# A hybrid decoder layer on one core: the input projection multiplies the raw rows, and the pooling sums run as a scan

## The chip, the cores and the metric

The kernel runs on one core of one Trainium2 chip. The metric is the device time of one execution in microseconds (us), lower is better; the time before is the median of three runs. The profile is one further execution, recorded by the hardware profiler.

## The reference, cut to what matters

One layer (`DEPTH` 1) over 512 rows (tokens) of width 1024: a root-mean-square norm, one wide projection, three mixers side by side (attention, causal pooling, a state-space scan), a merge, and a feed-forward part. The pooling windows w are 2, 4, 8 and 16, for 256 columns each. The change touches the norm, the pooling and the first uses of the projection:

```python
def rmsnorm(x, g):
    y = xf * lax.rsqrt(jnp.mean(xf * xf, axis=-1, keepdims=True) + NORM_EPS)
    return (y * g.astype(jnp.float32)).astype(x.dtype)
...
    u = rmsnorm(x, ln1_g[i])
    proj = u @ w_in[i]
    q, k, v, pool_in, z, xbc, dt_raw, gate_pre = jnp.split(proj, split_idx, axis=-1)
...
def pool_mixer(u, w_grp, scale):
    cs = jnp.cumsum(uf, axis=1)
    for gi, w in enumerate(POOL_WINDOWS):
        c = cs[..., sl]
        shifted = jnp.pad(c, ((0, 0), (w, 0), (0, 0)))[:, :s]
        cnt = jnp.minimum(pos, w).astype(jnp.float32)
        outs.append((c - shifted) / cnt - uf[..., sl])
```

The factor `rsqrt(...)` belongs to a row. It can be put on the row before the product with `w_in` or on the row of the result behind it; the two orders give the same product.

## The kernel before, in words

**Products.** Every float32 operand is split into a high part (a rounded copy) and a low part (what the rounding left). A product is three passes, high by high, high by low, low by high, in `mm3` (L230). Weights arrive by DMA as `raw`; ScalarE writes the high part `wh` (`cast`, L185) and VectorE the low part `wl` (`low`, L221, its line L217). There are two buffers for `raw`, three for `wh`, two for `wl`. A `Job` is one weight block with its products. At job n the loop at the end of the kernel (L1949) issues the low part of block n+1, the cast of n+2 and the load of n+3, and then the job's products. An output chunk of 128 features by 512 rows is 24 matmuls (8 slices of the inner dimension, three passes), and then its evacuation.

**Order.** The instructions of each engine run in the order in which the program issues them (`manual_schedule`, L104). Small pieces of work are generators in `running`; `step()` (L155) takes each one `yield` further, and is called once a chunk (once in two row blocks in the jobs for v). `after(n, it)` holds a piece back by n steps. So the position of a piece in an engine's queue is counted in steps.

**Buffers.** All tiles of 128x512 come from one pool of 52 (`T`, L106). PSUM has four banks "mm" for products (`MM`) and four "sm" for everything else (`SM`).

**Start.** The normed, transposed input is kept as `uh` (high) and `ul` (low), 8 slices of 128 features by 512 rows. For the first 256 rows (two blocks) the kernel sums the squares of a block, works out the factor and writes it on a diagonal (L1895); TensorE multiplies the block by it (`turn_scale`, L1882), which turns and scales it in one. ScalarE and VectorE then write `uh` and `ul` from PSUM (`turned`, L1851). Rows 256 to 511 are scaled in SBUF (L1919, L1921) and turned by plain transposes (L1932). Until the first product the chain is load, squares, factor, diagonal, turn, split. WARM matmuls on a tile of ones (L1825) run ahead of it.

**First two jobs.** The pooling's projection is four jobs of two chunks. The first two of these are issued by hand (`begin`, L1858): each half of the rows of each job by itself, so 192 matmuls of 256 columns (L1866). The other two go through the loop, with 512 columns a matmul (L239). Then come two jobs for v of the first attention group with the state-space step widths (`v_jobs`, L622, 400 columns), three jobs for q and k (`qk_jobs`, L692) and the pooling's own product (`pool_out_job`, L921).

**Pooling.** `pool_evac` (L895): ScalarE copies the chunk out of PSUM to `pu`; GpSimd doubles windows (add the tile shifted by 1, 2, 4, 8, with a copy of the first columns each, L904 and L905) and corrects the first columns by `ramp` (L907). Two steps later VectorE forms mean minus value (L913), ScalarE its high part (L915), VectorE its low part (L916).

`sums_of_u` (L403) adds `uh` and `ul` back together (L408) for sums that later jobs use. A table `col` of biases is turned by TensorE (`turn`, L505), and `parts_of_bias` prepares a table of attention biases.

Of the kernel before, what the change touches and what calls it, by code (L numbers as in the profile page):

```python
# [10 lines left out]
F32 = mybir.dt.float32  # L11
# [5 lines left out]
P = 128  # L17
S = 512
# [64 lines left out]
def trunk(ctx: ExitStack, tc, out, x, rel_bias, ln1_g, w_in, b_gate, w_a, pool_w, pool_scale, w_b,  # L83
# [318 lines left out]

    def sums_of_u(p):  # L403

        f = []
        for k in (2 * p, 2 * p + 1):
            f.append(T("uf"))
            dve.tensor_tensor(f[-1], uh[:, k, :].bitcast(F32), ul[:, k, :].bitcast(F32), OP.add)  # L408
# [206 lines left out]
        return plain(ap, 1) if g == 0 else perm(ap, g)  # L615

    dtr = cpool.tile([P, 4, SH], F32, name="dtr")

    both = cpool.tile([P, 4, 32 + HEADS], F32, name="nmls")
    V, QK, OT, NM, LS = {}, {}, {}, {}, {}  # L620

    def v_jobs(g):  # L622
        extra = SH if g == 0 else 0

        def parts(k0, k1):
            c = C_V + 384 * g
            r = [wsrc(w_in, k0, k1, c, c + 384)]
            if extra:
                r.append(wsrc(w_in, k0, k1, C_DT, C_DT + SH))
            return r  # L630

        def evac(tb, ps):
            t = T(f"v{g}")
            act.copy(t[:, :384], ps[:, :384])
            if extra:
                act.copy(dtr[:, tb, :], ps[:, 384:400])
            V[g, tb] = t

        return jobs_b(parts, 384 + extra, lambda k, tb: uh[:, k, tb * P:(tb + 1) * P],
                      lambda k, tb: ul[:, k, tb * P:(tb + 1) * P], KD, evac)  # L640

    def v_pair():

# [252 lines left out]
    def pool_evac(m, ps):  # L896
        g = m // 2
        w = 2 << g
        u = T("pu")
        act.copy(u, ps)  # L900
        cur, sh = u, 1
        while sh < w:
            nxt = T("psw")
            pool.tensor_tensor(nxt[:, sh:], cur[:, sh:], cur[:, :S - sh], OP.add)  # L904
            pool.tensor_copy(nxt[:, :sh], cur[:, :sh])  # L905
            cur, sh = nxt, sh * 2
        pool.tensor_tensor(cur[:, :w], cur[:, :w], ramp[:, g, :w], OP.mult)  # L907

        def later():
            yield  # L910
            yield
            d = T("pd")
            dve.scalar_tensor_tensor(d, cur, 1.0 / w, u, OP.mult, OP.subtract)  # L913
            dh, dl = T("pdh", F32R), T("pdl", F32R)
            act.copy(dh, d)  # L915
            dve.tensor_sub(dl, d, dh.bitcast(F32))  # L916
            DP[m] = (dh, dl)

        running.append(later())
# [892 lines left out]
    load_x(0, (sp, act))  # L1812
    act.dma_start(eye, c_eye)
    load_x(1, (sp, act))
    act.dma_start(g8[:KD, :P], ln1_g[0].rearrange("(k p) -> k p", p=P))
    dve.memset(ones.bitcast(F32), 1.0)
# [4 lines left out]
    first = [MM("pa") for _ in range(4)]  # L1821

    def warm_up(n):
        for i in range(n):
            pe.matmul(first[3][:, :P], ones.bitcast(F32), ones.bitcast(F32), start=True, stop=True)  # L1825

    fetch(weights[0], 2)
    fetch(weights[1])
# [8 lines left out]
    sp.dma_start(tri, c_tri)  # L1837
    rows_of_bias, parts_of_bias, second_table, residues_of_bias = bias_rows()

    def row_squares(tb, ss, n=1, eng=dve):  # L1840

        for i in range(n):
            squares(act, xin[tb + i, 0], ss[:, i:i + 1])
            squares(eng, xin[tb + i, 1], ss[:, n + i:n + i + 1])
        dve.tensor_tensor(ss[:, :n], ss[:, :n], ss[:, n:2 * n], OP.add)
        return ss[:, :n]

    def x_block(tb, k):
        return xin[tb, k // 4][:, (k % 4) * P:(k % 4 + 1) * P]

    def turned(k, lo, ps):  # L1851

        hh = uh[:, k, lo:lo + 256]
        act.mul(hh, ps, g1[:, k:k + 1])
        dve.scalar_tensor_tensor(ul[:, k, lo:lo + 256], ps, g1[:, k:k + 1], hh.bitcast(F32),
                                 OP.mult, OP.subtract)

    def begin(n, lo, hi, between=lambda early: None):  # L1858
        wh, wl = weights[n].split
        js = range(2)  # L1860
        order = [(wh, uh, k, j) for j in js for k in js]
        for k in range(2, KD + 2):
            order += [(wh, uh, k, j) for j in js if k < KD] + [(wh, ul, k - 2, j) for j in js]
        for part in (order, [(wl, uh, k, j) for j in (1, 0) for k in range(KD)]):
            for a, b, k, j in part:
                pe.matmul(first[2 * n + j][:, lo:hi], a[:, k, j * P:(j + 1) * P], b[:, k, lo:hi],  # L1866
                          start=a is wh and b is uh and k == 0, stop=a is wl and k == KD - 1)
            between(part is order)
        if hi == S:
            for j in range(2):  # L1870
                pool_evac(2 * n + j, first[2 * n + j])
                step()


    warm_up(WARM)
    diag = [T("diag") for _ in range(2)]
    banks = [SM("uT") for _ in range(4)]

    def bank(k):
        return banks[k % 4][:, (k // 4) * 256:(k // 4) * 256 + 256]  # L1880

    def turn_scale(tb, k):  # L1882
        pe.matmul(bank(k)[:, tb * P:(tb + 1) * P], x_block(tb, k), diag[tb][:, :P], start=True, stop=True)

    for tb in range(2):
        s0, s1, v, sq, r, rt = (small(n, [P, 1]) for n in ("s0", "s1", "v", "sq", "r", "rt"))
        squares(act, xin[tb, 0], s0)
        squares(dve, xin[tb, 1], s1)
        dve.tensor_scalar(v, s0, 1.0 / D, EPS, OP.mult, OP.add)
        act.activation(sq, s1, AF.Sqrt, bias=v, scale=1.0 / D)  # L1890
        dve.scalar_tensor_tensor(rt, s1, 1.0 / D, v, OP.mult, OP.add)
        dve.reciprocal(r, sq)
        dve.scalar_tensor_tensor(rt, r, rt, r, OP.mult, OP.mult)
        dve.tensor_scalar(rt, rt, -0.5, 1.5, OP.mult, OP.add)
        dve.tensor_scalar(diag[tb][:, :P], eye, r, rt, OP.mult, OP.mult)  # L1895
        if tb == 0:
            for k in range(KD):
                turn_scale(0, k)
    pe.transpose(first[2][:, :KD], g8[:KD, :P], eye[:KD, :KD])
    dve.tensor_copy(g1, first[2][:, :KD])  # L1900

    cast(weights[0], 2, other=dve)
    low(weights[0], 2, pool)
    for k in range(KD):
        turn_scale(1, k % 2 * 4 + k // 2)
    for k in range(KD):
        turned(k, 0, bank(k))
    cast(weights[1], 2)
    parts = lows(weights[1], 2)


    ss = row_squares(2, small("ss", [P, 4]), 2)
    next(parts)
    r = rstd_of(ss, 2, D)
    for tb in (2, 3):
        for h in range(2):
            t = xin[tb, h]
            if h:
                dve.tensor_scalar(t, t, r[:, tb - 2:tb - 1], None, OP.mult)  # L1919
            else:  # L1920
                act.mul(t, t, r[:, tb - 2:tb - 1])  # L1921
    next(parts)
    begin(0, 0, 256)

    def turns(early):
        if not early:
            return
        for k in range(4):
            banks[k] = SM("uT")
        for k in range(KD):  # L1930
            for tb in range(2):
                pe.transpose(bank(k)[:, tb * P:(tb + 1) * P], x_block(2 + tb, k), eye)  # L1932
        for k in range(KD):
            turned(k, 256, bank(k))

    begin(1, 0, 256, turns)
    turn()
    parts_of_bias()
    fetch(weights[2])
    fetch(weights[3])  # L1940
    begin(0, 256, S)
    cast(weights[2])
    low(weights[2])
    begin(1, 256, S)
    cast(weights[3])
    fetch(weights[4])


    n = 0  # L1949
    for job in jobs:  # L1950
# [2 lines left out]
            continue  # L1953
        while second:
            flush()
        if n >= 2:
            def prepare(n=n, later=False, spread=not job.once):

                def rest():
                    if n + 1 < len(weights):  # L1960
# [27 lines left out]
WARM = 12  # L1988

# [1 line left out]
_INS = ['x', 'rel_bias', 'ln1_g', 'w_in', 'b_gate', 'w_a', 'pool_w', 'pool_scale', 'w_b',  # L1991
# [26 lines left out]
```

## Time and profile before

| what | us |
|---|---|
| median of 3 runs (lowest, highest) | 1014.83 (1014.29, 1014.94) |
| profiled execution, its time | 1014.66 |
| its span in the trace | 1012.9 |
| TensorE busy (share of the span) | 1000.9 (99%) |
| VectorE | 734.6 (73%) |
| ScalarE | 527.0 (52%) |
| GpSimd | 153.3 (15%) |

In the lines of the profile PE is TensorE, PEld its weight loads, DVE VectorE, ACT ScalarE, POOL GpSimd, SP the engine that issues most DMAs. A group's line has line of code, engine, operation, output<-inputs, shapes, count, then busy time in us and the mean ns of one, then the idle time in front. A line of the timeline has the start, the time until the last of the run has ended, engine and operation, and in brackets the idle time before it and what ended that. A line of the chain of waits has start, length and what ran. A busy TensorE is not TensorE at its peak, since matmuls overlap.

### The profile page before, as it was taken

To read this page: it belongs to the slowest core of one execution; us is meant where nothing else is said; L and a number is where in the kernel's file an instruction comes from. 1 tells how busy PE (TensorE), PEld (TensorE's weight loads), DVE (VectorE), ACT (ScalarE), POOL (GpSimd) and SP (SyncE) were. 2 spreads that over 40 slices of the span, in tenths; PEclk is the share of its full clock that TensorE was granted. 3 is DMA by queue.
4 is the path that set the end of the run, shared out by engine and by line. 5 is a ranking of instruction groups with operands and counts; after the bars stand their busy time and mean duration, and the time that the engine had idled before them with its cause. 6 is when DMAs were issued, how large, how long until landed. Compare 5 with 4: busy or idle time off the path is not lost.

```text
span 1012.9 us, 13676 instructions
## 1 busy us (share of the span) xinstructions
PE 1000.9 (99%) x5360; PEld 853.6 (84%) x5360; DVE 734.6 (73%) x933; ACT 527.0 (52%) x894; POOL 153.3 (15%) x141
## 2 busy tenths in 40 slices
PE   8999999999999999999999999999999999999996
PEld 8998878999988888888888888898888888888885
DVE  6564768577767655776889888768778768685877
ACT  5433556454435566888576246554444434443454
POOL 1680010110000000000043501302111100121031
PEclk9999999999999999999999999999999999999999
DMA  8244270655352435552253754232252134542573
GB/s 246 81 105 136 86 206 5 175 165 146 94 166 81 115 95 142 142 132 62 82 153 117 219 188 88 82 125 85 91 201 83 46 117 149 178 115 73 146 180 111
DMA packets 117583, 126.76 MB, mean 125 GB/s; under 512 B 6771, under 2 KB 96438, under 8 KB 117519
## 3 DMA queue, kind: packets, MB, share of 16 engines
q1 hardware_dynamic: 111887, 116.39, 37.0%
q0 software_dynamic: 5040, 8.65, 5.4%
q8 instruction: 42, 0.69, 0.3%
q10 hardware_dynamic: 592, 0.86, 0.2%
q14 instruction: 22, 0.18, 0.1%
HBM read 121.30 MB, written 3.00 MB: 123 GB/s over the span
## 4 chain that ended last, share of the span: by engine, by line
PE 95%; DVE 3%; DMA 1%; issue 0%; ACT 0%; ACTq 0%
PE pa L239 36%; PE pu L239 23%; PE pb L239 9%; PE pd L239 8%; PE pqk L239 6%; PE pq L239 3%; PE pa L1866 2%; PE ps L781 1%; PE ppw L239 1%; PE po L829 1%; PE pt L815 1%; PE py L1114 1%; PE pu L1543 1%; DVE wl L217 1%; DMA xin<-in_x_dram 1%; PE pyo L1121 1%
## 5 line engine op out<-in xcount | busy, mean ns | idle before, releaser
L217 DVE TENSOR_TENSOR wl<-raw,wh 128x2048 fp32r<-128x2048 f32 (+3 forms) x86 | 205.9, 2394 | 42.3 <-ACT wh L195 33.9
L195 ACT CAST wh<-raw 128x1024 fp32r<-128x1024 f32 (+3 forms) x169 | 169.8, 1022 | 48.9 <-DVE raw L362 17.8
L1440 DVE SCALAR_TENSOR_TENSOR hc<-pu,fcol,hc 128x510 f32<-128x510 f32 x88 | 65.8, 748 | 53.1 <-ACT hc L1437 51.5
L239 PE MATMUL pa<-uh,wh 128*128 128x512 f32 (+1 forms) x368 | 88.8, 381 | 0.0
L239 PE MATMUL pa<-ul,wh 128*128 128x512 f32 (+1 forms) x368 | 86.8, 375 | 0.0
L239 PE MATMUL pa<-uh,wl 128*128 128x512 f32 (+1 forms) x368 | 86.8, 375 | 0.0
L239 PE MATMUL pu<-uh,wh 128*128 128x512 f32 (+1 forms) x352 | 83.6, 379 | 0.0
L239 PE MATMUL pu<-uh,wl 128*128 128x512 f32 (+1 forms) x352 | 83.5, 379 | 0.0
L239 PE MATMUL pu<-ul,wh 128*128 128x512 f32 (+1 forms) x352 | 83.5, 379 | 0.0
L239 PEld LDWEIGHTS pa<-ul,wh 128*128 128x128 f32 x368 | 66.7, 188 | 12.6
L239 PEld LDWEIGHTS pa<-uh,wl 128*128 128x128 f32 x368 | 66.7, 188 | 12.5
L239 PEld LDWEIGHTS pa<-uh,wh 128*128 128x128 f32 x368 | 65.3, 189 | 11.8
L239 PEld LDWEIGHTS pu<-ul,wh 128*128 128x128 f32 x352 | 64.2, 188 | 12.5
L239 PEld LDWEIGHTS pu<-uh,wl 128*128 128x128 f32 x352 | 64.2, 188 | 12.5
L239 PEld LDWEIGHTS pu<-uh,wh 128*128 128x128 f32 x352 | 64.1, 188 | 12.4
L1445 POOL TENSOR_TENSOR hc<-hc 128x512 f32<-128x512 f32 x22 | 29.9, 1360 | 279.3 <-DVE hc L1440 243.3
L1437 ACT ACTIVATE hc<-pu,fcol,fcol 128x512 f32<-128x512 f32 x40 | 31.2, 779 | 75.0 <-PE pu L239 75.0
L217 DVE TENSOR_TENSOR wl<-w,wh 128x2048 fp32r<-128x2048 f32 (+1 forms) x26 | 54.2, 2087 | 10.3 <-issue 4.6
L195 ACT CAST wh<-w 128x1024 fp32r<-128x1024 f32 (+1 forms) x52 | 47.2, 950 | 10.0 <-DVE x L1666 5.3
L803 ACT ACTIVATE sb<-sb,nmls 128x128 f32<-128x128 f32 (+1 forms) x72 | 30.0, 418 | 31.6 <-DVE nmls L800 20.9
L1097 POOL TENSOR_TENSOR st<-st,dts 128x512 f32<-128x512 f32 x4 | 4.2, 1050 | 225.5 <-ACT st L1105 165.6
L1442 ACT ACTIVATE hc<-hc 128x512 f32<-128x512 f32 x22 | 13.9, 632 | 40.3 <-DVE hc L1440 40.2
(436 smaller groups left out, 1964.4 us busy)
## 6 DMA issues: line engine op xcount, KB each, us to landing
raw<-in_w_in_dram SPq DMA_DIRECT2D x24, 1024.0 KB, 5.5
raw<-in_ffn_w_up_dram SPq DMA_DIRECT2D x22, 1024.0 KB, 5.1
raw<-in_w_in_dram SPq DMA_DIRECT2D x14, 512.0 KB
raw<-in_w_in_dram SPq DMA_DIRECT2D x8, 768.0 KB, 7.3
raw<-in_ffn_w_down_dram SPq DMA_DIRECT2D x6, 1024.0 KB, 5.1
raw<-in_w_b_dram SPq DMA_DIRECT2D x4, 1024.0 KB, 5.3
al<-ad SPq DMA_DIRECT2D x16, 256.0 KB, 6.8
raw<-in_w_c_dram SPq DMA_DIRECT2D x4, 1024.0 KB, 7.6
```

The lines of the kernel that those rows point to most:

```text
L195: (other.tensor_copy if other and i else act.copy)(job.high[:, :, o], job.raw[:, :, o])
L217: (eng or dve).tensor_tensor(l[:, :, o], job.raw[:, :, o], h[:, :, o].bitcast(F32), OP.subtract)
L239: pe.matmul(ps, l, r, start=first and n == 0, stop=last and n == total - 1, skip_group_check=onto)
L781: pe.matmul(pss[i][:, o:o + w * P], q[r, n * P:(n + 1) * P], k[r, kb * P:(kb + w) * P], start=True, stop=True)
L803: act.activation(sb[:, off:off + w * P], sb[:, off:off + w * P], AF.Exp, bias=nm[:, n, h:h + 1], accum_out=ls[:, n, h:h + 1])
L815: pe.transpose(pt[:, o:o + P], sb[:, o:o + P], eye)
L829: pe.matmul(po[DH * hh:DH * hh + DH, n * P:(n + 1) * P], V[g, kb + i][:, (2 * c + hh) * DH:(2 * c + hh + 1) * DH], probs[2 * c + hh, nb][: ...
L1437: act.activation(t, ps, AF.Identity, bias=ff["c1"][:, ff["b"] + m:ff["b"] + m + 1], scale=fw(2, m))
L1440: dve.scalar_tensor_tensor(t[:, sh:], ps[:, :S - sh], fw(k, m), t[:, sh:], OP.mult, OP.add)
L1442: act.activation(t, t, AF.Silu)
L1445: pool.tensor_tensor(a, a, t, OP.mult)
L1866: pe.matmul(first[2 * n + j][:, lo:hi], a[:, k, j * P:(j + 1) * P], b[:, k, lo:hi], start=a is wh and b is uh and k == 0, stop=a is wl and ...
```

## The change

1. The rows are turned as loaded: 32 plain transposes into PSUM, no diagonal. ScalarE and VectorE write the high and low parts `xh`, `xl` of x times the gain, one block of 128 rows and one slice at a time (`split_x`), in the order `TURN` = 0, 4, 1, 5, 2, 6, 3, 7, so that the two slices of one PSUM bank follow each other. `x_parts` takes 24 of the 52 tiles: `xh`, `xl`, `xf`.
2. The four pooling jobs and the two jobs for v multiply `xh`, `xl`. The rows' factor comes behind: as a row in all partitions (`rows["r"]`, by way of a transpose, a write to DRAM and a broadcast load) in `pool_evac`, and as a column (`rcol`) in the evacuation of v. The sums of squares move behind the splits.
3. Job 0 alone is issued by hand, both high-part passes ahead of the low part of the weights. Its weights arrive in two halves ahead of the other rows; VectorE casts the first half, ScalarE the second, GpSimd writes the low parts. Job 1 goes through the loop with 512 columns a matmul.
4. `pool_evac`: VectorE multiplies the chunk by the factor out of PSUM, and makes the running sum of the window by two scans, one over the first w columns, one that adds the new column and subtracts the one that leaves. Mean minus value comes four steps later, its low part a step after that.
5. `uh` and `ul` are written later, in `normed`: GpSimd multiplies `xf` (x times gain, whole) by the row of factors, ScalarE copies to `uh`, VectorE subtracts to `ul`, spread over ten steps. `xf` itself is written by GpSimd (first 256 rows) and ScalarE (others, from PSUM). `sums_of_u` of the first four slices uses `xf` and no longer adds.
6. The turn of `col` and `parts_of_bias` run in steps inside job 1 and job 2. WARM is 10 in place of 12.

The diff, cut:

```diff
     def sums_of_u(p):
-        f = []
-        for k in (2 * p, 2 * p + 1):
-            f.append(T("uf"))
-            dve.tensor_tensor(f[-1], uh[:, k, :].bitcast(F32), ul[:, k, :].bitcast(F32), OP.add)
+        if p < 2:
+            f = [xf[2 * p], xf[2 * p + 1]]
+        else:
...
+    def normed():
+        for k in range(0, KD, 2):
+            for i in (k, k + 1):
+                pool.tensor_tensor(xf[i], xf[i], rows["r"], OP.mult)
+                act.copy(uh[:, i, :], xf[i])
+            yield
+        yield
+        for k in range(0, KD, 2):
+            yield
+            for i in (k, k + 1):
+                dve.tensor_sub(ul[:, i, :], xf[i], uh[:, i, :].bitcast(F32))
     def v_jobs(g):
...
-            act.copy(t[:, :384], ps[:, :384])
+            act.mul(t[:, :384], ps[:, :384], rcol[:, tb:tb + 1])
...
     def pool_evac(m, ps):
         u = T("pu")
-        act.copy(u, ps)
-        cur, sh = u, 1
-        while sh < w:
-            nxt = T("psw")
-            pool.tensor_tensor(nxt[:, sh:], cur[:, sh:], cur[:, :S - sh], OP.add)
-            pool.tensor_copy(nxt[:, :sh], cur[:, :sh])
-            cur, sh = nxt, sh * 2
-        pool.tensor_tensor(cur[:, :w], cur[:, :w], ramp[:, g, :w], OP.mult)
+        dve.tensor_tensor(u, ps, rows["r"], OP.mult)
+        cur = T("psw")
+        dve.tensor_tensor_scan(cur[:, :w], ones.bitcast(F32)[:, :w], u[:, :w], 0.0, OP.mult, OP.add)
+        dve.tensor_tensor_scan(cur[:, w:], u[:, w:], u[:, :S - w], cur[:, w - 1:w], OP.add, OP.subtract)
+        dve.tensor_tensor(cur[:, :w], cur[:, :w], ramp[:, g, :w], OP.mult)
         def later():
+            for _ in range(4):
+                yield
+            dve.scalar_tensor_tensor(cur, cur, 1.0 / w, u, OP.mult, OP.subtract)
...
+            act.copy(dh, cur)
             yield
+            dve.tensor_sub(dl, cur, dh.bitcast(F32))
...
-        yield from jobs_a(w_in, C_POOL, 8, uhk, ulk, KD, pool_evac)
+        yield from jobs_a(w_in, C_POOL, 8, xhk, xlk, KD, pool_evac)
...
     act.dma_start(g8[:KD, :P], ln1_g[0].rearrange("(k p) -> k p", p=P))
+    sp.dma_start(eye, c_eye)
+    load_x(0, (act, sp))
...
+    load_x(1)
+    load_w0(0, 0, 8)
+    load_w0(1, 0, 8)
     load_x(2)
     load_x(3)
+    fetch(w1)
...
+    def turned(tb):
+        if tb % 2 == 0:
+            banks[:] = [SM("uT") for _ in range(4)]
+        o = tb % 2 * P
+        for k in TURN:
+            pe.transpose(bank(k)[:, o:o + P], xin[tb, k // 4][:, (k % 4) * P:(k % 4 + 1) * P], eye)
+
+    def split_x(tb, k):
+        o, c = tb % 2 * P, slice(tb * P, (tb + 1) * P)
+        act.mul(xh[k][:, c], bank(k)[:, o:o + P], g1[:, k:k + 1])
+        dve.scalar_tensor_tensor(xl[k][:, c], bank(k)[:, o:o + P], g1[:, k:k + 1],
+                                 xh[k][:, c].bitcast(F32), OP.mult, OP.subtract)
...
     warm_up(WARM)
     pe.transpose(first[2][:, :KD], g8[:KD, :P], eye[:KD, :KD])
+    turned(0)
     dve.tensor_copy(g1, first[2][:, :KD])
+    for k in TURN:
+        split_x(0, k)
+    turned(1)
+    for n, k in enumerate(TURN):
+        if n == 2:
+            for k0 in (0, 4):
+                dve.tensor_copy(h0[part(0, k0, k0 + 4)], raw0[part(0, k0, k0 + 4)])
+            low0(0, 0, KD)
+        split_x(1, k)
+    group(0, (HH,), 0, 256, TURN)
+    group(0, (HL,), 0, 256, TURN)
+    for k0 in (0, 4):
+        act.copy(h0[part(1, k0, k0 + 4)], raw0[part(1, k0, k0 + 4)])
+    low0(1, 0, KD)
...
+    group(1, (HH,), 0, 256)
+    turned(2)
+    for k in TURN:
+        split_x(2, k)
+    group(1, (HL,), 0, 256)
+    group(0, (LH,), 0, 256)
...
+    turned(3)
+    for k in TURN:
+        split_x(3, k)
+    group(1, (LH,), 0, 256)
+    fetch(weights[2])
...
+    both_high(256, S, (0, 1))
+    group(0, (LH,), 256, S)
+    group(1, (LH,), 256, S)
...
+    dve.tensor_tensor(ss[:, :4], ss[:, :4], ss[:, 4:], OP.add)
+    r = rstd_of(ss[:, :4], 4, D)
+    for j in range(2):
+        act.copy(w1.high[:, :, j * P:(j + 1) * P], w1.raw[:, :, j * P:(j + 1) * P])
+    dve.tensor_copy(rcol, r)
+    pe.transpose(first[2][:4, :P], rcol, eye)
...
+    sp.dma_start(rd.rearrange("(t p) -> t p", p=P), rt[:4, :P])
+    sp.dma_start(rows["r"], rd.partition_broadcast(P))
+    low(w1, 2)
+    cast(weights[2], 2)
+    fetch(weights[3])
     for k in range(KD):
+        act.mul(xf[k][:, 256:], bank(k), g1[:, k:k + 1])
     low(weights[2])
+    running.append(after(3, columns_of(turn)))
+    running.append(after(4, columns_of(parts_of_bias)))
+    for j in range(2):
+        pool_evac(j, first[j])
+        step()
+    running.append(normed())
```

More of the change, by code (lines that the diff above doesn't have):

```diff
@@ L1838, in trunk @@
     rows_of_bias, parts_of_bias, second_table, residues_of_bias = bias_rows()
[L1840 to L1872, printed above, removed]
@@ L1875, in trunk, with part, low0 @@
-    warm_up(WARM)
-    diag = [T("diag") for _ in range(2)]
-    banks = [SM("uT") for _ in range(4)]
+    h0 = w0.high = whp.tile([P, KD, 256], F32R, name="wh", tag="wh")
+    l0 = wlp.tile([P, KD, 256], F32R, name="wl", tag="wl")
+    w0.split = h0, l0
+    def part(j, k0, k1):
+        return slice(None), slice(k0, k1), slice(j * P, (j + 1) * P)
+    def low0(j, k0, k1):
+        o = part(j, k0, k1)
+        pool.tensor_tensor(l0[o], raw0[o], h0[o].bitcast(F32), OP.subtract)
+    banks, TURN = [], (0, 4, 1, 5, 2, 6, 3, 7)
@@ new lines, in split_x, with columns_of, mm @@
+    def split_x(tb, k):
[3 more added lines that the diff above has]
+                                 xh[k][:, c].bitcast(F32), OP.mult, OP.subtract)
+    def columns_of(turn):
+        turn()
+        return
+        yield
+    opened = set()
+    def mm(j, w, b, k, lo, hi, last=False):
+        pe.matmul(first[j][:, lo:hi], w[:, k, j * P:(j + 1) * P], b[k][:, lo:hi],
+                  start=j not in opened, stop=last, skip_group_check=True)
+        opened.add(j)
@@ new lines, in group, with both_high, half_squares @@
+    def group(j, pairs, lo, hi, ks=range(KD)):
+        for w, b in pairs:
+            for k in ks:
+                mm(j, w, b, k, lo, hi, w is l0 and k == KD - 1)
+    HH, HL, LH = (h0, xh), (h0, xl), (l0, xh)
+    def both_high(lo, hi, js):
+        for n in range(KD + 1):
+            for w, b, i in ((h0, xh, n), (h0, xl, n - 1)):
+                if 0 <= i < KD:
+                    for j in js:
+                        mm(j, w, b, TURN[i], lo, hi)
+    ss = small("ss", [P, 8])
+    def half_squares(eng, tb, h):
+        i = 4 * h + tb
+        squares(eng, xin[tb, h], ss[:, i:i + 1])
@@ L1899, in trunk @@
+    warm_up(WARM)
     pe.transpose(first[2][:, :KD], g8[:KD, :P], eye[:KD, :KD])
+    turned(0)
     dve.tensor_copy(g1, first[2][:, :KD])
-    cast(weights[0], 2, other=dve)
-    low(weights[0], 2, pool)
-    for k in range(KD):
-        turn_scale(1, k % 2 * 4 + k // 2)
-    for k in range(KD):
[L1907 to L1941, printed above, removed]
```

81 lines of the change are left out of this document (42 added, 39 removed).

## The prediction, made before the changed kernel ran

> **What bounds the kernel now.** I read the page first: the busy shares and the chain that ended last.
>
> ```profile
> PE 1000.9 (99%) x5360; PEld 853.6 (84%) x5360; DVE 734.6 (73%) x933; ACT 527.0 (52%) x894; POOL 153.3 (15%) x141
> PE 95%; DVE 3%; DMA 1%; issue 0%; ACT 0%; ACTq 0%
> ```
>
> TensorE sets the time: 99% busy and 95% of the chain. The change can win only where TensorE does not yet multiply, at the start, or where it does the same product in less time. It loses wherever TensorE is made to wait, because no slack behind gives the time back. So next the chain of waits in order of time, the first part and two pieces further on.
>
> ```profile
> 1.66 6.14 DMA xin<-in_x_dram
> ...
> 9.99 2.05 PE uT L1883 x16
> 12.04 9.60 PE pa L1866 x80
> 21.64 1.75 PE uT L1932 x16
> 23.39 1.92 PE pa L1866 x16
> 25.30 0.12 issue
> 25.43 0.27 PE colp L508
> 25.70 11.55 PE pa L1866 x96
> 37.25 21.79 PE pa L239 x96
> ...
> 77.56 32.64 PE pqk L239 x144
> ```
>
> Up to about 12 us the chain is load, squares, factor, diagonal, turn; behind that TensorE alone, with no gap but the 0.12 us at 25.30. The reader should see the two prices of one product: L1866 takes 11.55 / 96 = 0.120 us for 256 columns, so 0.240 for 512, while L239 takes 21.79 / 96 = 0.227 for 512. The timeline gives the first product and what stands before it:
>
> ```profile
> 1.06 4.96 PE L1825 MATMUL pa<-ones 128*128 128x128 f32 x24 [1.06 <-DVE ones L1816]
> 1.19 0.45 ACTq L1813 DMA_DIRECT2D eye<-in_c_eye_dram  x1
> 8.81 0.22 PE L1899 MATMUL pa<-eye,g 8*128 8x8 f32 x1
> 9.86 0.16 DVE L1900 COPY g<-pa 128x8 f32<-128x8 f32 x1
> 9.93 0.68 DVE L195 CAST wh<-raw 128x1024 fp32r<-128x1024 f32 x1
> 11.80 0.96 PE L1866 MATMUL pa<-uh,wh 128*128 128x256 f32 x6
> ```
>
> **The change part by part.** The sum is made against the profiled execution (1014.66 us; span 1012.9, so 1.8 lie around the span); the median of the runs, 1014.83, is 0.2 above it.
>
> *The new start.* These groups give the prices:
>
> ```profile
> L1084 ACT ACTIVATE al<-al,acs 128x128 f32<-128x128 f32 x64 | 20.4, 389 | 3.7 <-DMA al<-ad 3.7
> L1854 ACT ACTIVATE uh<-uT,g 128x256 fp32r<-128x256 f32 x16 | 6.3, 483 | 2.4 <-PE uT L1932 1.5 <-PE uT L1883 0.9
> L195 ACT CAST wh<-raw 128x1024 fp32r<-128x1024 f32 x141 | 145.0, 1044 | 32.6 <-DMA raw<-in_w_c_dram 13.4 <-DVE raw L344 11.6 <-DVE raw L362 3.0
> L1127 DVE SCALAR_TENSOR_TENSOR xs<-xs,dgc,ea 128x128 f32<-128x128 f32 x24 | 6.8, 348 | 0.2
> L442 DVE SCALAR_TENSOR_TENSOR junk<-xin 128x512 f32<-128x512 f32 x4 | 3.4, 876 | 4.5 <-DMA xin<-in_x_dram 4.5
> 18.37 0.16 DVE L425 TENSOR_SCALAR v<-ss 128x2 f32<-128x2 f32 x1
> 19.65 0.16 DVE L434 TENSOR_TENSOR r<-rt,r 128x2 f32<-128x2 f32 x1
> GB/s 0 33 164 377 307 314 370 314 291 330 346 350 374 387 355 109 75 61 233 375 378 35 1 155 360 386 146 0 0 16 0 0 0 0 0 0 0 15 180 396
> ```
>
> A split of 128 columns costs ScalarE about 0.30 us (20.4 / 64 = 0.32 from SBUF; 6.3 / 16 = 0.39 for 256 columns out of PSUM) and VectorE 0.28 (6.8 / 24). The 10 warm-up matmuls end at 1.06 + 4.96 x 10/12 = 5.2. The gain's transpose and its copy (0.22 and 0.16, L1899 and L1900) with their hand-overs add 0.5, so ScalarE splits from 5.7 and has its 16 pieces of the first two blocks at 5.7 + 16 x 0.30 = 10.5. VectorE follows about 0.45 behind; after ten pieces, at 5.7 + 3.0 + 0.45 = 9.15, it casts the first half of the weights, as much as L195's 0.68 us in two pieces with some overhead, 0.8: 9.95. The first product can start at 10.0, against 11.8.
>
> Do the loads cover that? The last line is the traffic of each us from 0. Block 0, block 1 and the first half of the weights (0.52 MB each) are 1.6 MB with the unit matrix. By 7 us 1.57 MB had come before; one DMA now stands before x on each of its queues (0.45 us of issue, L1813), so that is 7.6 to 8, over a us of cover. If x or the half came 2 us later, the gain would be gone.
>
> Behind 10.0 TensorE has 96 matmuls of 256 columns (11.55) and 16 transposes (1.75 to 1.9), 13.4 us, to 23.4. Their inputs come in time by the same prices: the last low part of the first two blocks at 9.95 + 6 x 0.285 = 11.7 where it is wanted at 11.9; the second half of the weights on ScalarE (L195, 1.04) at 10.5 + 1.1 = 11.6; blocks 2 and 3 are split by 16 and 19.8, and TensorE, at 0.48 us a slice, walks behind them from 17.7. Behind 19.8 VectorE has one square (0.9, L442; 1.4 beside GpSimd), an add and the factor's chain (L425 to L434, 1.4): 22.3 to 23.0. One transpose of the factor (0.12) waits on that with TensorE's whole queue behind it, so its slack is 0.4 us or more. Job 1 starts at 23.6 and takes 48 x 0.227 = 10.9, to 34.5. Before, the same two jobs were done at 37.25. The turn of `col`, 0.4 with its gap, comes back later inside the stream at 0.15 to 0.3. The sum: 11.8 - 10.0 = 1.8 for the start, 96 x 0.120 - 48 x 0.227 = 0.65 for job 1 in full width, 0.1 to 0.25 for `col`, 0.15 back for the factor's transpose: 2.4 to 2.55.
>
> *The factor as a row.* It travels to DRAM and back; the bias rows show such a trip.
>
> ```profile
> 70.20 0.63 SPq L547 DMA_DIRECT2D rdram<-rv  x2
> 72.17 1.40 SPq L556 DMA_DIRECT2D b<-rdram  x3
> b<-rdram SPq DMA_DIRECT2D x3, 256.0 KB, 3.8
> ```
>
> The second write is issued at about 70.5 and the read behind it at 72.17, 1.7 us; 3.8 to land: 5.5 us, so the row is there at 24.2 + 5.5 = 29.7. VectorE, busy with low parts until 29.0, waits 0.7 us. Queued behind it are the pooling chunks; TensorE isn't, since job 1's two chunks go into the two "mm" banks that job 0 doesn't hold, and job 2 wants the first of those at 34.7. On SP nothing urgent stands behind the row: the load of block 3's weights, wanted at 45.
>
> *VectorE's new work.* ScalarE's copy (8) and GpSimd's sums leave; VectorE gets the multiply and the scans. Prices:
>
> ```profile
> L408 DVE TENSOR_TENSOR uf<-uh,ul 128x512 f32<-128x512 f32 x8 | 5.1, 684 | 0.0
> L217 DVE TENSOR_TENSOR wl<-raw,wh 128x1024 fp32r<-128x1024 f32 x2 | 2.4, 1218 | 0.0
> L217 DVE TENSOR_TENSOR wl<-raw,wh 128x1536 fp32r<-128x1536 f32 x11 | 19.3, 1753 | 4.9 <-PE pq L239 2.5 <-PE pb L239 1.4 <-ACT wh L195 0.8
> L866 DVE RECIPROCAL dtmp<-den 6x512 f32<-6x512 f32 x1 | 3.3, 3332 | 0.0
> L904 POOL TENSOR_TENSOR psw<-pu 128x511 f32<-128x511 f32 x8 | 8.3, 1037 | 17.2 <-ACT pu L900 17.2
> 36.70 0.68 DVE L913 SCALAR_TENSOR_TENSOR pd<-psw,pu 128x512 f32<-128x512 f32 x1
> 47.45 1.50 DVE L913 SCALAR_TENSOR_TENSOR pd<-psw,pu 128x512 f32<-128x512 f32 x1 [0.36 <-POOL psw L907]
> ```
>
> The trace has no scan. Its lower bound is one pass, 0.68 us; its upper bound the slowest operation of 512 columns, 3.33. I take 1.2: L217 gives (1753 - 1218) / 512 = 1.045 ns an element and 0.15 fixed, and since each sum has to pass an add and a subtract before the next element can start, I count two element times, 0.15 + 510 x 2.09 ns = 1.2. That is nearer to the lower bound, because the scan is a plain pass in all else. With a multiply of 0.68 (L408) and two small operations of 0.2 an evacuation is 2.3 us, eight are 18.3. The Trainium skill ("DVE: opcode table, instruction layouts, handler registers and perf-mode slots", section 6) says that the built-in `tensor_tensor_scan` runs at half throughput, since its result goes back to an earlier stage. This speaks against the change; no trace here shows it; by that rule the scan is the 1.2 above, and at full rate VectorE would have 8 x 0.53 = 4.2 us less to do.
>
> Is VectorE then late for TensorE? From 24.0 to the last low part `ul` that TensorE wants, in the first q and k job (77.56 - 2.45 = 75.1 for its start, high by low from 76.9, slice 6 at 78.3), VectorE has: low parts of six blocks, by L217's line, 3 x 2.3 + 2.4 + 2 x 1.8 = 12.9; evacuations 18.3; differences and their low parts, 13 x 0.68 = 8.9; eight `ul` 5.5; small ones about 2: 47.6 us in 54.3. Of the 6.7 left 0.7 go for the row, and 1 or 2 for chunks that aren't done yet. GpSimd's eight multiplies (L904's kind, 8.4 us) meet VectorE in job 1 and 2; an operation that met GpSimd took 1.50 in place of 0.68, and if 3 to 6 do, 2.5 to 5 us go. So it comes out about even at worst; I take no wait, and 0 to 2 us as the bounds. Edits at nothing: ScalarE's extra copies and multiplies (L1854's prices, 8 x 0.4 and 8 x 0.6, while ScalarE was half idle), the later `bias` work and four adds less.
>
> The forecast is 2.3 us off, a tenth or two kept back: 1014.66 - 2.3 = 1012.36, against the median 1012.5.
>
> **The rivals.**
>
> *VectorE gives part back.* The scan at 1.6 to 2.0, or every meeting with GpSimd at the full 0.8, and the first q and k job waits 0.5 to 2.3 us for `ul`. For it: 6 us of slack over 54 are thin, and steps put the last `ul` at the very end of the v jobs. Against: VectorE's list as priced above ends before that. 1012.8 to 1014.8.
>
> *The scan makes VectorE the bound (slower).* A us more for each scan is 8 us more ahead of `ul`. With 6 us of slack (the waits for chunks end as the scan grows) it starts to cost at 1.2 + 6/8 = 1.95 us; the gain is gone at 1.2 + 8.3/8 = 2.25; at 3.3 TensorE waits 17 - 6 = 11 us, 1023. Place: the low-part matmuls of the first q and k job. For it: the upper bound. Against: a running sum has two simple operations.
>
> *The clock falls in the start.* In the new order TensorE idles between the last turn of block 1 (about 8.9) and the first product.
>
> ```profile
> 1006.00:1009.00 3.00, 0.00 (x0) 0.00 (x0) 2.79 (x11) 2.35 (x5) 0.00 (x0) 0.97 0.32 120
> 1009.00:1013.00 4.00, 0.00 (x0) 0.00 (x0) 0.03 (x1) 0.00 (x0) 0.00 (x0) 0.50 0.58 217
> ```
>
> At the end, with no matmul after 1006, the granted clock (third number from the right) is 0.97 in the first 3 us and 0.50 in the next 4. If the first half of the weights came 2 to 3 us late, the idle time would reach that: products start at 12 or 13 and some 3 us of them run at half speed, 1015 to 1017. Against: a cover of over a us, and idle spans of 1 us leave the clock alone now.
>
> *It doesn't start earlier.* The turn of block 1 waits bank by bank for both readers of block 0; if that doubled the splits, products would start at 11.8 and only 0.65 remain: 1014.
>
> **How the numbers follow.** A measurement of this kernel tells 0.2%, 2.0 us, from no change, so faster means below 1012.8. The forecast, 0.65: within 0.7 of 1012.5, three quarters of it below the bound. Part given back or no earlier start, 0.17: nearly all within the bound. The scan as bound, 0.11, and the clock, 0.04: slower, but for 0.02. Something not seen, 0.03, slower. Faster 0.65 x 0.75 + 0.02 = 0.51, slower 0.16, same 0.33. The range leaves out 0.07 below 1011.6 and 0.12 above 1015.3; the forecast's own is 1011.8 to 1013.2.
>
> **What would show it.** Right: the first product at about 10, no gap to job 1 at about 23.6, job 1 at 0.227 us a matmul, the first q and k job at about 75.1 and no wait of TensorE on `ul`; scans of 1.2 us; some 20 us of GpSimd in the first 80. Wrong: a wait of TensorE for `rcol`, `ul`, `xl` or a bank; a scan of over 1.95; a granted clock under 1.00 before 12 us; a first product after 11.

## The result: 0.64% slower

The changed kernel takes 1021.45 us (median of 6 runs, 1020.88 to 1022.21), the kernel before 1014.78 beside it: a ratio of 1.0064, 95% interval 1.0054 to 1.0075. Forecast were 1012.5, with 1015.3 as the upper end. The profiled execution took 1021.05 us with a span of 1018.9.

The page of the changed kernel, busy shares and chain by engine:

```profile
PE 1003.8 (99%) x5293; PEld 851.8 (84%) x5293; DVE 755.1 (74%) x972; ACT 533.5 (52%) x919; POOL 132.8 (13%) x109
PE 94%; DVE 4%; ACT 1%; issue 0%
```

Shares of a whole span hardly show it: TensorE still at 99%, its part of the chain 94% instead of 95%, VectorE's 4 instead of 3. The chain in order of time does. Its start and two pieces further on (start, length, what ran):

```profile
5.72 0.38 PE uT L1895 x2
6.13 0.38 ACT xh L1899
6.53 0.36 DVE xl L1900
6.92 0.38 ACT xh L1899
7.32 0.62 DVE xl L1900 x2
7.96 0.38 ACT xh L1899
...
14.91 0.38 ACT xh L1899
15.33 3.90 PE pa L1911 x17
19.22 0.23 PE uT L1895 x2
19.48 0.38 ACT xh L1899
...
28.63 1.23 ACT junk L443 x4
...
31.76 0.27 PE pa L1984
32.03 10.91 PE pa L239 x48
...
83.40 32.64 PE pqk L239 x144
```

Before, TensorE ran alone from 9.99 us. Now the chain goes to and fro between ScalarE (`xh`) and VectorE (`xl`) for two long stretches, 6.1 to 15.3 and 19.5 to 28.6, with one pair of pieces every 1.04 us (6.92 to 7.96). Job 1 starts at 32.03, where 23.6 was forecast. The first product came at 12.33, not at 10.0. Behind the start nothing is lost: job 1 takes its 10.91, and the first q and k job starts 51.4 us behind job 1 (forecast: 51.5).

What ScalarE waits for, in its timeline, and the waits of TensorE up to 130 us (total, times, longest):

```profile
6.92 0.63 ACT L1899 ACTIVATE xh<-uT,g 128x128 fp32r<-128x128 f32 x2 [0.42 <-DVE xl L1900]
...
PE uT L1895 <- DVE xl L1900: 3.5, 6, 1.0
...
PE pa L1911 <- DVE wh L1945: 0.8, 1, 0.8
...
PE pa L1984 <- DVE rcol L1983: 0.2, 1, 0.2
```

ScalarE makes two pieces in 0.63 us and then stands 0.42 until VectorE has finished one. The two pieces run on from one another where they lie in two banks (slices 4 and 1, 5 and 2, ...); the wait comes between the two slices of one bank (0 and 4, 1 and 5, ...). `TURN` puts these in succession: VectorE needs the piece's `xh` before it can write `xl`, and ScalarE may read the bank's other half only when VectorE has left the bank. So the engines work in turn, in what is called lock step below.

The granted clock of TensorE (third number from the right; the first ones are the stretch, its length and the busy times):

```profile
8.00:10.00 2.00, 1.03 (x5) 0.48 (x4) 1.20 (x4) 1.22 (x4) 0.00 (x0) 0.68 1.19 306
10.00:12.00 2.00, 1.19 (x4) 0.39 (x3) 1.13 (x5) 1.25 (x4) 0.00 (x0) 0.50 1.04 383
...
18.00:20.00 2.00, 2.00 (x16) 2.00 (x15) 0.12 (x1) 0.37 (x1) 2.00 (x3) 0.76 0.09 8
```

It falls at about 8.7 us (0.68 as a mean of 1.00 and 0.50) and comes back at about 19 (0.76). The 17 products at 15.33, high parts and low parts that had become ready, take 3.90 us; at the 0.120 us of the kernel before they would be 2.0.

### The profile page after: what moved, and what is told of

It is laid out like the page before. It is cut to its first block, busy times and chain, and to the rows that moved or that the text cites. A ratio compares the mean times of both kernels' runs of the same rounds, so it can differ in the third digit from the quotient of the medians.

```text
span 1018.9 us, 13576 instructions
## 1 busy us (share of the span) xinstructions
PE 1003.8 (99%) x5293; PEld 851.8 (84%) x5293; DVE 755.1 (74%) x972; ACT 533.5 (52%) x919; POOL 132.8 (13%) x109
## 4 chain that ended last, share of the span: by engine, by line
PE 94%; DVE 4%; ACT 1%; issue 0%
PE pa L239 37%; PE pu L239 22%; PE pb L239 9%; PE pd L239 7%; PE pqk L239 6%; PE pq L239 3%; PE ps L810 1%; PE ppw L239 1%; PE po L858 1%; DVE xl L1900 1%; PE py L1140 1%; PE pt L844 1%; PE pu L1569 1%; ACT xh L1899 1%; DVE wl L217 1%; PE pyo L1147 1%
## 5 line engine op out<-in xcount | busy, mean ns | idle before, releaser
L195 ACT CAST wh<-raw 128x1024 fp32r<-128x1024 f32 (+2 forms) x168 | 167.0, 1011 | 53.4 <-DVE raw L362 17.8
L1466 DVE SCALAR_TENSOR_TENSOR hc<-pu,fcol,hc 128x510 f32<-128x510 f32 x88 | 65.9, 749 | 53.0 <-ACT hc L1463 51.4
L239 PE MATMUL pa<-uh,wh 128*128 128x512 f32 (+1 forms) x336 | 80.9, 380 | 0.0
L239 PE MATMUL pa<-ul,wh 128*128 128x512 f32 (+1 forms) x336 | 78.9, 374 | 0.0
L239 PE MATMUL pa<-uh,wl 128*128 128x512 f32 (+1 forms) x336 | 78.8, 374 | 0.0
L239 PEld LDWEIGHTS pa<-ul,wh 128*128 128x128 f32 x336 | 60.7, 188 | 11.3
L239 PEld LDWEIGHTS pa<-uh,wl 128*128 128x128 f32 x336 | 60.7, 188 | 11.2
L239 PEld LDWEIGHTS pa<-uh,wh 128*128 128x128 f32 x336 | 59.4, 189 | 10.6
```

What stands on the lines that cost most here:

```text
L195: (other.tensor_copy if other and i else act.copy)(job.high[:, :, o], job.raw[:, :, o])
L239: pe.matmul(ps, l, r, start=first and n == 0, stop=last and n == total - 1, skip_group_check=onto)
L1466: dve.scalar_tensor_tensor(t[:, sh:], ps[:, :S - sh], fw(k, m), t[:, sh:], OP.mult, OP.add)
```

## The experiments

Two explanations stood against each other for the slow splits. L: two pieces of one PSUM bank in succession go in lock step, so the order is the cause. H: a piece of 128 columns simply costs 0.5 us, in any order. C is about the clock: what its fall costs beside this.

**Order 0 to 7.** The changed kernel with splits and products in slice order, turns as they were:

```diff
-    for k in TURN:
+    for k in range(KD):
         split_x(...)
-    group(0, (HH,), 0, 256, TURN)
+    group(0, (HH,), 0, 256)
```

> The changed kernel, only the order of the pieces of x is other: ScalarE and VectorE split slices 0, 1, 2 ... 7 (a new PSUM bank with each piece) in place of 0, 4, 1, 5 ... (two pieces of one bank behind each other). Theory L (lock step: the program lets one engine read a bank only when the other has read it, so that a pair of pieces costs 1.05 us and not 2 x 0.30): the 16 pieces of the first two blocks end at about 11 and not at 15.3, first product at 10 to 10.5, job 1 starts at 23.6 with a full clock or up to 2.5 us later with a clock that falls all the same; 1012.5 to 1015 us. Rival H (a piece of 128 columns costs 0.5 us in any order, since VectorE needs ScalarE's result): no change, 1021.4 us.

Measured: 1013.41 (10 runs, 1012.68 to 1014.88), ratio to before 0.999 (0.998 to 0.9999). ScalarE's timeline and the chain:

```profile
6.55 4.30 ACT L1899 ACTIVATE xh<-uT,g 128x128 fp32r<-128x128 f32 x14 [3.29 <-PE uT L1895]
10.68 4.58 PE pa L1911 x24
...
25.74 10.91 PE pa L239 x48
```

Fourteen pieces in one row, 0.31 us each, with no wait between them, and 8.0 us less time. L holds and H falls. The 24 products still took 4.58, since the clock fell in this execution (0.50 from 12 to 14 us). Over the runs the times stand in two groups, seven at 1012.7 to 1013.6 and three at 1014.7 to 1014.9; the profiled one is of the upper group. Two of these three have a longer span (1012.7 and 1012.8) and a mean clock of 0.996; the third has a span of 1011.3 like the seven, so its extra lies around the span.

**Idle matmuls, order kept.** The changed kernel with six matmuls on the tile of ones:

```diff
+        if tb == 1: warm_up(0)
         for k in TURN:
+            if tb == 1 and k < 4: warm_up(1)
             pe.transpose(...)
...
     turned(1)
+    warm_up(2)
```

> The changed kernel in its own order, with six idle matmuls of the warm-up kind more, put where TensorE waits in the turn of block 1 (one ahead of each bank, two behind). Theory C (TensorE is too idle there, the granted clock falls to 0.50 from 8.8 to 19 us, and 17 products at half speed lie on the path): the clock stays at 1.00, the 17 products behind 15.3 take 2.0 us and not 3.9; 1019.5 us. If the fall of the clock is hidden behind the splits: 1021.4 us.

Measured: 1020.93 (4 runs), ratio 1.0063 (1.0048 to 1.0078), only 0.5 less. The clock held to 14 us and then fell (0.53 from 14 to 16), so 17 products still took 3.41. The 1019.5 expected was missed: the fill did not hold the clock, so this run does not give its price.

**More idle matmuls, order kept.** As before, and besides:

```diff
     turned(1)
-    warm_up(2)
+    warm_up(3)
...
-    group(0, (HH,), 0, 256, TURN)
+    for n, k in enumerate(TURN):
+        mm(0, h0, xh, k, 0, 256)
+        if n % 2 and n < 7: warm_up(2)
```

> The changed kernel in its own order (0, 4, 1, 5, ...), with more idle matmuls at the start: one ahead of each bank of the turn of block 1, three behind that turn, two behind each of the first three pairs of job 0's products. Theory C (behind the lock step the clock falls because TensorE has too little to do between 8 and 18 us, and the 17 products in a row at about 15 us run at half speed): clock near 1.00 from 8 us on, the 17 products in 2.0 us instead of 3.9, 1019.3 to 1019.8. If the clock costs nothing, since the splits of blocks 2 and 3 end no earlier: 1021 to 1021.6, at a full clock.

Measured: 1019.91 (4 runs), ratio 1.0051 (1.0035 to 1.0068), 1.5 less than the changed kernel. The windows and the chain:

```profile
8.00:10.00 2.00, 1.32 (x8) 0.94 (x8) 1.13 (x5) 1.25 (x4) 0.00 (x0) 1.00 1.18 302
16.00:18.00 2.00, 2.00 (x19) 2.00 (x18) 0.52 (x2) 1.80 (x6) 1.36 (x1) 1.00 0.19 49
15.59 2.29 PE pa L1915 x17
...
30.91 10.93 PE pa L239 x48
```

Clock at 1.00, the same 17 products in 2.29 us instead of 3.90: C holds, 0.1 us above the times expected. The clock's fall is about 1.5 us of the loss.

**Order 0 to 7 with five idle matmuls.** The edit of the order 0 to 7, and

```diff
+        if tb == 1: warm_up(3)
         for k in TURN:
             pe.transpose(...)
...
     turned(1)
+    warm_up(2)
```

> Both: slices in the order 0 to 7, and five idle matmuls more (three ahead of the turn of block 1, two behind). Theories L and C together: first product at 10 to 10.5 at full clock, job 1 at 23.6 to 24, 1012.5 us, at most 1013.5. If the clock doesn't fall in the first experiment, the same time as there.

Measured: 1013.19 (10 runs, 1012.99 to 1013.70), ratio 0.9986 (0.9977 to 0.9995): faster than both kernels, and the upper group of times is gone. The chain:

```profile
2.60 6.96 DMA raw<-in_w_in_dram
...
9.58 0.44 DVE wh L1950
...
10.16 3.46 PE pa L1915 x24
...
24.09 10.91 PE pa L239 x48
```

The first product is 0.16 later than the prediction's 10.0 and waits for another reason, the first half of the weights, which landed at 9.56.

**Half the order.** The same, but blocks 2 and 3 again in `TURN`.

```diff
-    for k in range(KD):
+    for k in TURN:
         split_x(2, k)
...
-                        mm(j, w, b, i, lo, hi)
+                        mm(j, w, b, TURN[i], lo, hi)
```

> The kernel with slice order 0 to 7 and five idle matmul groups (1013.19), where only blocks 2 and 3 (their splits and the products that use them) go back to the order 0, 4, 1, 5, .... Theory L (each pair of pieces of one bank takes 1.05 us in place of 0.60): blocks 2 and 3 have 8 pairs, 8 x 0.45 = 3.6 us more for the splits, part of it hidden under products that are there anyway: 1016 to 1017, so about half of the 8 us lies in each half of the start. If the second half is hidden: 1013 to 1013.5, and all of the 8 us lie ahead of the first product.

Measured: 1015.52 (10 runs), ratio 1.001 (1.0 to 1.0019), 2.3 more. Job 1 starts at 26.57, 2.48 later:

```profile
26.57 10.91 PE pa L239 x48
```

So the loss of 8.3 us (1021.45 against 1013.19) splits in three: 1.5 clock (1021.45 to 1019.91), 4.4 lock step of blocks 0 and 1 (1019.91 to 1015.52), 2.3 lock step of blocks 2 and 3. The kernels compared differ in their idle matmuls too, so the split is rough. The second half came out below the 1016 to 1017 expected: more of its 3.6 us was hidden.

**The order in the kernel before.** Its splits of 256 columns and its first products in `TURN`, nothing else:

```diff
-    for k in range(KD):
+    for k in (0, 4, 1, 5, 2, 6, 3, 7):
         turned(k, 0, bank(k))
```

> The kernel before, with only the order of its splits and products in the first two jobs changed to 0, 4, 1, 5, 2, 6, 3, 7. Theory L: a pair of its pieces of 256 columns goes from 0.82 us to about 1.3, so each set of eight takes some 1.9 us more; the first set lies on the path, the second half hidden: 1016.5 to 1018.5 us. Rival H: no change, 1014.8 us.

Measured: 1016.92 (8 runs), ratio 1.0025 (1.0015 to 1.0036), 2.3 slower. First ScalarE's eight pieces in the kernel before, in one row; then the chain with the other order, where the two engines take turns, now with 256 columns:

```profile
10.74 3.27 ACT L1854 ACTIVATE uh<-uT,g 128x256 fp32r<-128x256 f32 x8 [0.89 <-PE uT L1883]
...
10.90 0.48 ACT uh L1854
11.41 0.49 DVE ul L1855
11.93 0.48 ACT uh L1854
12.43 0.89 DVE ul L1855 x2
```

The order alone makes the old kernel slower too, so the cause isn't tied to the new start.

**Order or place.** Is it the order, or that neighbours in it share a bank? The changed kernel, order untouched, with the n-th slice of the order in bank n mod 4:

```diff
-        return banks[k % 4][:, (k // 4) * 256:(k // 4) * 256 + 256]
+        n = TURN.index(k)
+        return banks[n % 4][:, (n // 4) * 256:(n // 4) * 256 + 256]
```

> The changed kernel with its order 0, 4, 1, 5, ... of turns, splits and products left as it is, and only the place of the slices in PSUM changed: the slice that comes n-th goes to bank n mod 4, so pieces that follow each other lie in different banks, and two of one bank stand four pieces apart. Theory L (the lock step comes from two successive pieces lying in one bank, not from the order as such): pieces at 0.30 us as with the order 0 to 7, first product at about 10.7, job 1 at 25.7 or, where the clock holds, 24.1; 1012.7 to 1014.9 as there (1013.41). If the order itself is what costs (the halves of x, or TensorE's order of products): the time stays at 1021.

Measured: 1016.77 (10 runs), ratio 1.0019 (1.0009 to 1.0028): 4.7 less, but 3.4 above the order 0 to 7. Only half of the gain expected came; ScalarE's timeline and the chain:

```profile
6.70 2.17 ACT L1900 ACTIVATE xh<-uT,g 128x128 fp32r<-128x128 f32 x8 [3.44 <-PE uT L1896]
9.97 1.66 ACT L1900 ACTIVATE xh<-uT,g 128x128 fp32r<-128x128 f32 x6 [1.11 <-PE uT L1896]
...
8.53 1.42 PE uT L1896 x5
...
11.46 5.29 PE pa L1912 x24
```

The pieces are at 0.27 us, without lock step. But ScalarE stands 1.11 us ahead of block 1, behind five turns. With slices of one bank now four apart, TensorE writes to the first bank again with its fifth turn, and a reader of the bank waits for both. The clock is in it too: it was 0.50 from 10 to 16 us, so the 24 products took 5.29, where they take 3.46 at 1.00.

**Place and order of the turns.** The same, with TensorE's turns by pairs of a bank:

```diff
-        for k in TURN:
+        for k in (0, 2, 4, 6, 1, 3, 5, 7):
             pe.transpose(...)
```

> The kernel with the slices' other place in PSUM (1016.77), where only TensorE's order of turns changes, to 0, 2, 4, 6, 1, 3, 5, 7: the two slices of one bank are turned in succession, while the splits still come 0, 4, 1, 5, ... in other banks. Theory: a reader of a bank also waits until TensorE has written both slices of it, so there the splits of each block waited for five turns instead of two (ScalarE 1.11 us ahead of block 1); with pairs the first split comes behind two turns, 14 pieces in a row at 0.30 us, first product at 10.7, and the time that of the order 0 to 7 (1013.4; 1012.7 to 1014.9, by whether the clock falls). Rival (the rest of the loss is the clock alone, which had fallen at 9.7 us): first product still at 11.4, 1016 to 1017.

Measured: 1013.02 (10 runs, 1012.59 to 1014.89), ratio 0.9986 (0.9976 to 0.9995). Timeline of ScalarE and chain:

```profile
5.73 3.98 ACT L1900 ACTIVATE xh<-uT,g 128x128 fp32r<-128x128 f32 x14 [2.47 <-PE uT L1896]
9.54 3.46 PE pa L1912 x24
...
23.47 10.91 PE pa L239 x48
...
74.82 32.64 PE pqk L239 x144
```

This kernel, called the repaired one below, keeps the change's order 0, 4, 1, 5, ... of splits and products and reaches the forecast's times along the way: first product at 9.54 (10.0), job 1 at 23.47 (23.6), the q and k job at 74.82 (75.1). This execution took 1012.59, the least of the ten; one of them (1014.89, mean clock 0.996) was in the upper group. With the five idle matmuls besides:

```diff
+        if tb == 1: warm_up(3)
         for k in (0, 2, 4, 6, 1, 3, 5, 7):
...
     turned(1)
+    warm_up(2)
```

> The same with the five idle groups (three ahead of the turn of block 1, two behind). Theory: clock 1.00 throughout, first product at about 10.1, job 1 at 24.1, 1013.0 to 1013.4, the time of the order 0 to 7 with the same idle groups (1013.19), so the order of splits and products is worth nothing once banks no longer repeat. If the order itself costs: over 1014.

Measured: 1013.03 (10 runs, 1012.77 to 1013.61), ratio 0.9985 (0.9976 to 0.9994), as expected. So the order of splits by itself is worth nothing. What costs is that successive pieces share a bank, and that a bank's turns stand apart; either the order or the place mends the first.

**Scans alone.** The kernel before with its running sums as two scans on VectorE, ScalarE's copy kept:

```diff
-        cur, sh = u, 1
-        while sh < w: ...            # doubling on GpSimd
-        pool.tensor_tensor(cur[:, :w], cur[:, :w], ramp[:, g, :w], OP.mult)
+        cur = T("psw")
+        dve.tensor_tensor_scan(cur[:, :w], ones.bitcast(F32)[:, :w], u[:, :w], 0.0, OP.mult, OP.add)
+        dve.tensor_tensor_scan(cur[:, w:], u[:, w:], u[:, :S - w], cur[:, w - 1:w], OP.add, OP.subtract)
+        dve.tensor_tensor(cur[:, :w], cur[:, :w], ramp[:, g, :w], OP.mult)
```

> The kernel before, with only the pooling's running sums moved to VectorE as two scans and the ramp's multiply with them; ScalarE's copy and all else stay. In the changed kernel the scans took 1.25 us alone and 2.27 beside GpSimd, and VectorE ended its last low part before TensorE wanted it. The theory (what the changed kernel lost it lost at its start, and the scans cost nothing): scans of 1.25 us, since GpSimd has little left there, no wait of TensorE on VectorE in the first 110 us, 1014.2 to 1015.2. Rival (the scans delay TensorE by way of the low parts of the weights that stand behind them on VectorE): over 1016, with waits of TensorE at the v, q or k jobs.

Measured: 1014.53 (10 runs) beside 1014.54, ratio 0.9998 (0.9989 to 1.0008). Here GpSimd has no multiplies beside the scans, and the largest takes 1.28 us:

```profile
L903 DVE TENSOR_TENSOR_SCAN psw<-pu,psw 128x510 f32<-128x510 f32 x2 | 2.6, 1281 | 0.1
```

The scans neither cost nor gain time.

**x first.** The order 0 to 7 with five idle matmuls, and block 0 of x loaded ahead of gain and unit matrix:

```diff
+    load_x(0, (act, sp))
     act.dma_start(g8[:KD, :P], ...)
-    sp.dma_start(eye, c_eye)
-    load_x(0, (act, sp))
+    act.dma_start(eye, c_eye)
```

> The kernel with slice order 0 to 7 and five idle matmul groups (1013.19), where block 0 of x is loaded first on both queues and the gain and the unit matrix behind it on ScalarE's queue. If x's landing (5.46 us) bounds the first product (10.16): x 0.4 us earlier, first product at 9.8, 1012.7 to 1012.9. If the unit matrix, now behind it, or the first half of the weights (its cast waited until 9.56) bounds: 1013.2 or more, and the first product at 10.1 or later.

Measured: 1014.88 (10 runs, 1013.98 to 1016.58), ratio 1.0 (0.9991 to 1.001), 1.7 worse. The chain:

```profile
1.80 4.91 DMA eye<-in_c_eye_dram
...
11.26 3.47 PE pa L1915 x24
```

The unit matrix, now behind x, landed at 6.72 and held TensorE 1.2 us.

## Why the prediction was wrong, step by step

**The step that failed** is "a split of 128 columns costs ScalarE about 0.30 us ... 16 pieces of the first two blocks at 10.5". The prices were right, 0.27 to 0.31 on either engine in the kernels without lock step; the addition was wrong. It put the pieces of each engine in one row, each engine waiting for the other's data alone, 0.45 behind. That holds while successive pieces lie in different banks, as the kernel before had it. `TURN` stood in the diff with two slices of one bank side by side, and with that each pair costs ScalarE and VectorE in turn: 1.04 us instead of 0.60. The 16 pieces of the first two blocks took from 6.13 to 15.3, 9.2 us instead of 4.8; 0.67 of it is VectorE's cast of the weights, which now stands in the chain. (The pieces also began 0.4 later than the 5.7 forecast, since the warm-up ended at 5.57 and not at 5.2.) That a bank's two readers take turns in this program is what the waits show; whether the chip would bear them at once was not tried. The Trainium skill ("PSUM — Partial Sum Buffer", section "PSUM bank collisions raise a hardware error") says that it would not: two engines on one bank at once collide, reads against reads included, and a kernel should guard by bank and not by address. The waits here go by that rule, a writing TensorE against a reader as well (the 1.11 us of ScalarE behind five turns).

**Rivals.** "It doesn't start earlier" named the place, the bank and both readers, but only for the turn of block 1, and priced it at a start of 11.8 and 1014. It left out that the splits themselves go in step, that blocks 2 and 3 pay again (2.3 us), and that the clock follows. "The clock falls in the start" was right in its effect and wrong in its cause: no weights came 2 to 3 us late; the lock step spread TensorE's work over a longer time, and more work in the gaps held the clock. It is worth about 1.5 us. Neither the scan as the bound nor VectorE giving back a part came to pass.

**The loads.** "7.6 to 8, over a us of cover" for the first half of the weights was too early, for the order 0 to 7 with idle matmuls at least: there it landed at 9.56, and VectorE's cast waited 0.29 us for it. In the repaired kernel the cast began at 8.97 without a wait. So the loads kept up, but without the cover of a us.

**Factor and job 1.** The factor's transpose was to have 0.4 us of slack. In the changed kernel the factor is on the chain (28.63 to 32.03), since the splits of block 3 end at 28.6 and not at 19.8; in the repaired kernel TensorE doesn't wait for it. Job 1 at full width took 10.91, as worked out.

**The row of factors** was to take 5.5 us. It took 4.8: the write issued at 32.37, the multiply that waits for the row free at about 37.1. VectorE idled 0.31 for it (forecast 0.7):

```profile
32.37 0.25 SPq L1988 DMA_DIRECT2D rows<-rowsT  x1
...
37.13 0.69 DVE L929 TENSOR_TENSOR pu<-pa,rows 128x512 f32<-128x512 f32 x1 [0.31 <-DMA rows<-rows]
```

**The scan** was to take 1.2 us; groups of the changed kernel, by shape, one of GpSimd's, and VectorE's last `ul`:

```profile
L932 DVE TENSOR_TENSOR_SCAN psw<-pu,psw 128x496 f32<-128x496 f32 x2 | 2.5, 1252 | 0.1
...
L932 DVE TENSOR_TENSOR_SCAN psw<-pu,psw 128x510 f32<-128x510 f32 x2 | 4.6, 2278 | 0.1
...
L933 DVE TENSOR_TENSOR psw<-psw,ramp 128x2 f32<-128x2 f32 x2 | 2.2, 1076 | 0.1
...
L642 POOL TENSOR_TENSOR xf<-xf,rows 128x512 f32<-128x512 f32 x8 | 11.9, 1521 | 13.0 <-ACT xf L1994 13.0
...
83.06 1.27 DVE L649 TENSOR_TENSOR ul<-xf,uh 128x512 fp32r<-128x512 f32 x2
```

Alone it takes 1.25 to 1.28, two element times as worked out, which bears out the half throughput of the Trainium skill's page cited there. In the first 12 us of evacuations, beside GpSimd's multiplies, it takes 2.28, above the 1.95 from which the rival was to start; but only three of the eight meet it, and the smallest operations go from 0.16 to as much as 1.08. Together that is about 6 us against the 2.5 to 5 reckoned. VectorE's last `ul` ended at 84.33, 0.9 behind the start of the q and k job and ahead of its use, and TensorE did not wait.

**What remains.** The repaired kernel's ten runs have a median span of 1010.9, the kernel before beside them 1012.7: 1.8 less, where 2.3 was forecast. (The profiled execution's 1010.5 comes to the forecast, but it is the fastest of the ten: that agreement is luck.) In the median times it is 1.5 (1013.02 against 1014.55). The 0.3 between is time around the span: 2.1 in the kernels with the new start (2.0 to 2.2 in all but two runs), where before it was 1.8. It came with the change and not with the scans (1014.36 less 1012.6 is 1.8), and its cause is open. So is that of the missing 0.5; runs of one kernel differ by as much, and x's first block landed at 5.21 to 5.88 in the profiles whose chain shows it.

## What to carry to other kernels

A price for one piece holds for a row of pieces only if successive pieces share nothing, so look up in which PSUM bank each lies before adding them up: in this program two readers of one bank took turns, and a reader waited for all of the bank's writes that were issued ahead of it. Let the writer finish a bank at a time, and let the two readers go from bank to bank. And look at the granted clock where TensorE gets its work in small portions: here the next 17 products took 3.90 us instead of 2.29.

## What the runs showed of the hardware

The clock fell without a long idle stretch, and a share of busy time does not tell when: in the changed kernel TensorE was recorded busy for 1.02 us from 6 to 8 and for 1.03 from 8 to 10, its longest wait for a bank was 1.0, and the clock went to 0.68 in the second of these stretches and to 0.50 behind it. With more idle matmuls, at 1.25 and 1.32, it stayed at 1.00. But the kernel before was busy for 1.19 and 1.04 in the same stretches and the repaired kernel for 0.77 and 1.25, and both stayed at 1.00. The second stretch of the kernel before:

```profile
8.00:10.00 2.00, 1.04 (x10) 0.83 (x9) 1.69 (x10) 1.23 (x2) 0.00 (x0) 1.00 1.17 311
```

So no threshold follows from these traces; that work in the gaps helps is shown by the runs with idle matmuls alone. Going by span and mean clock, the clock fell in two of ten runs with the order 0 to 7 and in one of ten of the repaired kernel, and with the five idle matmuls in none of either. The Trainium skill ("TensorE: Matmul & The Clock Gate", section "What's actually happening") has a window of about 3.4 us that runs freely, which fits the two groups of times; that the clock falls after an idle window fits less well, since TensorE was at work about half of the time. No run here varied the window's phase.

GpSimd's multiplies, which read two tiles, stretched a scan of 510 columns from 1.28 us (the scans alone) to 2.28, and a multiply of two columns from 0.16 to 1.08. The Trainium skill ("SBUF — State Buffer", section "Who interferes with whom") says that a VectorE instruction with two inputs in SBUF contends with a GpSimd instruction that reads SBUF; the scan behaves as such a one.
